# A hybrid decoder block on one core: the down projection's weights multiplied by the modulation's row during the attention and kept in DRAM; the residual's correction behind two products of the first down step

## The chip, the cores and the metric

One core of one Trainium2 chip (trn2) runs the whole block in one program. The metric is device time in microseconds (us). The engines are named as in the profile: PE (TensorE, matrix products), DVE (VectorE), ACT (ScalarE), POOL (GpSimd), SP (SyncE, here the queue that issues nearly all DMAs).

## The reference

The block has 1024 tokens of width 1024, one sequence, and everything is float32. A conditioning vector gives six rows of 1024 numbers; two of them, g1 and g2, scale what is added to the residual.

```python
cond = jax.nn.silu(c)
mod = (cond @ w_ada[l] + b_ada[l])[:, None, :]
sh1, sc1, g1, sh2, sc2, g2 = jnp.split(mod, N_ADA, axis=-1)

h = modulate(rmsnorm(x, norm1_g[l]), sh1, sc1)
u, q, k, v, gate_a, gate_b = jnp.split(h @ w_in[l], IN_SPLITS, axis=-1)
y_a = s5_branch(u, ...) @ w_a[l]
y_b = stick_breaking_attention(q, k, v) @ w_b[l]
merged = (jax.nn.sigmoid(gate_a) * y_a + jax.nn.sigmoid(gate_b) * y_b) @ w_o[l]
x = x + g1 * merged

h = modulate(rmsnorm(x, norm2_g[l]), sh2, sc2)
ffn = (jax.nn.silu(h @ w_ffn_gate[l]) * (h @ w_ffn_up[l])) @ w_ffn_down[l]
x = x + g2 * ffn
return rmsnorm(x, norm_f_g)
```

The hidden width of the FFN is 2816 = 22 x 128, so `w_ffn_down` is 22 tiles of 128 x 1024. Because g2 is a row over the output columns, `g2 * (a @ w)` equals `a @ (w * g2)`: the kernel multiplies the weights.

## The kernel before, in words

**Products in three passes.** Most float32 operands are split into a high part (a copy to a shorter float format, on ACT) and a low part (the difference, on DVE or POOL); a product is then three PE passes, high-high, high-low and low-high (`PRODUCTS`). `operand` does such a split for a tile of 128 x 1024 and takes the two result tiles from a ring that turns: two entries of pool `w`, one of `wg`, one of `wx`. In the down projection four tiles of pool `f` join the ring.

**Order.** The program is traced in Python and then ordered by a planner: an instruction may go to its engine as soon as the planner's own simulation has its inputs ready and its buffer free, earlier lines first among those that are ready. On each engine the resulting order is fixed, and an instruction that has to wait holds up everything behind it on that engine (DMA issues on SP too). In the attention the PE products are pinned to their program order (`pinned`); `self.after` adds an order between two instructions by hand.

**The attention** (`attention`) goes over 40 units, each a block of keys against 512 queries for a pair of heads: `scores` (products, then exponent and logarithm on ACT, splits on DVE at L875 to L877), `sums` (running sums over keys with a carried row, L898 to L902) and `values`. Between them PE is fed from `fillers`: 14 projections (q, k and gate) of 48 products, whose weights are loaded two projections ahead and split with the help of POOL (L454, L455).

**The modulation's columns.** The products of the conditioning vector with `w_ada` are made as partial sums per partition on DVE (`ada_rest`, L966 to L978) and stored as `aD`; the columns 8 to 11 are made in `branch_a`, 10 and 11 being g2. `ada_row` turns two such columns into a row on all partitions: load, split, products with a matrix of ones, and the bias added.

**The FFN** is one level of a seven-product scheme (Winograd's): matrices are cut into two by two blocks, sums of blocks are multiplied, and the seven products are added up with signs. `gate_up` does it for 11 pairs of hidden tiles and stores what the down projection needs of the hidden blocks as `hD`. At pair 8 it also makes the row g2 (L1178, L1179).

**The down projection** (`down`) handles the first 20 weight tiles in three steps of 4, 3 and 3 pairs (`STEPS`), each with seven products in the order (2, 4, 5, 3, 1, 6, 7); the last two tiles are added at the end, row block by row block. For each step it loads the weight tiles and multiplies them by the row on POOL:

```python
nc.sync.dma_start(out=w, in_=w_v[m])
nc.gpsimd.tensor_tensor(w, w, g2, ALU.mult)      # L1308
```

For each of the seven products and each pair, a stage tile gets the hidden block (a load from `hD`, L1329) and the sum or difference of two weight blocks (POOL, L1337), and is split by ACT and DVE (L1338, L1339). A product whose weight operand is a single block (2 and 5) needs no sum; its halves are split directly (L1334, L1335). One product of a four-pair step is 48 PE matmuls (L1354) into four banks.

The results are gathered in seven accumulators `acc`. Four of them (4, 5, 7, 6) start from the residual x, loaded from `xD` (L1295); in the first step the products 2, 3 and 1 are copied into theirs (half by ACT, half by DVE), the others are added by DVE (L1360). Since 4 and 5 also start from the residual and are later added and subtracted when the blocks are put together, accumulator 7 is corrected before: 7 plus 5 minus 4, four POOL operations on 128 x 1024 (L1298), traced ahead of the first step. In the last step POOL puts the blocks together (`closing`, L1315); the last rows are normalized and stored.

## Time and profile before

| | |
|---|---|
| median of 3 runs | 1498.04 us (1497.13 to 1499.16) |
| the profiled execution's own time | 1498.89 us |
| span of that profile | 1497.2 us |
| granted TensorE clock over the span | 0.976 |
| PE, DVE, ACT, POOL busy | 1414.6, 1125.6, 621.6, 504.3 us |

By the span's stretches: the state-space branch and the first projections to about 300 us, the merge of that branch (`branch_a`) to 370, the attention to about 668, its merge and the output product to 840, the up product of the FFN to 1253, the down projection to the end. A line of the profile such as "L1308 POOL TENSOR_TENSOR pa<-pa,row 128x1024" names the source line, the engine, the operation, the result and the operands by the program's tile names; "idle before, releaser" says how long the engine waited before it and what ended the wait. Weight tiles of the down projection are `pa`, the accumulators `pb` and `x`, the row g2 is `row`.

### The profile page before, as it was taken

How to read it: one execution, taken by the hardware profiler on the slowest of the kernel's cores; microseconds unless marked ns; L12 is line 12 of the kernel's file. 1: busy time of each engine (PE TensorE's matmuls, PEld its weight loads, DVE VectorE, ACT ScalarE, POOL GpSimd, SP SyncE). 2: the span in 40 equal slices, each digit the busy share in tenths (PEclk: the TensorE clock that was granted, in tenths of full speed). 3: DMA queues.
4: the chain of work that ended last, by engine and by line, in shares of the span. 5: the costliest groups of instructions: out<-in, count | busy, mean ns of one | idle time of the engine just before them, and what ended most of it. 6: DMA issues, size and time to landing. Idle time of an engine off the chain costs nothing.

```text
span 1497.2 us, 18257 instructions
## 1 busy us (share of the span) xinstructions
PE 1414.6 (94%) x6706; PEld 1118.1 (75%) x6706; DVE 1125.6 (75%) x1523; ACT 621.6 (42%) x804; POOL 504.3 (34%) x266
## 2 busy tenths in 40 slices
PE   5898999999999999999998799999999998999995
PEld 3678888787666666668887588888888886888774
DVE  5878995456797989868637866666666669999997
ACT  3321122632587776764236433333333333433323
POOL 1000000102111111104300245444555468888795
PEclk9999999999999999999999899999999999999998
DMA  9556665579011112136533233333333346455312
GB/s 340 134 110 163 151 175 134 158 258 333 27 49 50 35 37 77 50 106 218 183 108 107 81 106 106 106 106 106 106 106 106 106 174 220 143 160 175 100 50 113
DMA packets 180409, 193.55 MB, mean 129 GB/s; under 512 B 28636, under 2 KB 130080, under 8 KB 180320
## 3 DMA queue, kind: packets, MB, share of 16 engines
q1 hardware_dynamic: 171184, 184.86, 39.3%
q10 hardware_dynamic: 8912, 7.48, 1.8%
q8 instruction: 53, 0.87, 0.2%
q14 instruction: 36, 0.29, 0.1%
q0 software_dynamic: 224, 0.05, 0.0%
HBM read 142.40 MB, written 48.76 MB: 128 GB/s over the span
## 4 chain that ended last, share of the span: by engine, by line
PE 61%; DVE 20%; issue 6%; DMA 5%; ACT 4%; POOL 3%; SPq 0%; DVEq 0%; ACTq 0%; POOLq 0%
PE tq L1255 11%; PE mm L1255 5%; PE wo L1255 5%; PE mx L807 5%; PE mm L807 4%; PE ga L733 4%; PE tq L1354 3%; PE acc L807 2%; PE mm L1112 2%; PE mm L641 2%; DMA aw<-in_w_ada_dram 2%; PE z L807 2%; PE wo L1112 2%; PE mm L733 2%; PE tq L1112 1%
## 5 line engine op out<-in xcount | busy, mean ns | idle before, releaser
L471 POOL TENSOR_TENSOR ws<-wb 128x1024 f32<-128x1024 f32 x26 | 64.2, 2470 | 181.1 <-PE tq L1158 78.1
L455 POOL TENSOR_TENSOR wl<-ws,wh 128x1024 fp32r<-128x1024 f32 x12 | 31.2, 2601 | 161.2 <-ACT wh L452 151.8
L900 DVE TENSOR_TENSOR wa<-wa,acc 128x512 f32<-128x512 f32 (+1 forms) x80 | 47.0, 628 | 32.6 <-ACT row L898 30.2
L1308 POOL TENSOR_TENSOR pa<-pa,row 128x1024 f32<-128x1024 f32 x22 | 64.1, 2939 | 2.2 <-DMA pa<-in_w_ffn_down_dram 2.2
L294 POOL MEMSET tz<- 128x1024 f32 x4 | 3.8, 953 | 179.4 <-PE mm L641 96.7
L1246 POOL TENSOR_TENSOR f<-f,f 128x512 f32<-128x512 f32 x30 | 50.0, 1693 | 31.4 <-DVE f L1236 22.9
L872 ACT ACTIVATE ws<-wa 128x1024 f32<-128x1024 f32 (+1 forms) x40 | 39.1, 976 | 48.5 <-DVE wa L869 43.3
L471 POOL TENSOR_TENSOR wgs<-wb 128x1024 f32<-128x1024 f32 x14 | 34.6, 2474 | 72.4 <-DVE wgl L474 30.3
L877 DVE TENSOR_TENSOR wl<-ws,wh 128x1024 fp32r<-128x1024 f32 (+1 forms) x40 | 57.1, 1427 | 1.0
L977 DVE SCALAR_TENSOR_TENSOR acc<-aw,cond,acc 128x512 f32<-128x512 f32 x56 | 43.8, 782 | 7.8 <-DMA aw<-in_w_ada_dram 6.9
L875 DVE SCALAR_TENSOR_TENSOR ws<-wa,ws 128x1024 f32<-128x1024 f32 (+1 forms) x40 | 45.5, 1136 | 4.9 <-ACT ws L874 3.9
L1354 PE MATMUL tq<-f,f 128*128 128x512 f32 x156 | 48.2, 390 | 0.2 <-DVE f L1339 0.2
L1235 ACT ACTIVATE f<-f 128x1024 f32<-128x1024 f32 x22 | 23.3, 1061 | 59.8 <-DVE f L1277 30.4
L903 ACT ACTIVATE wa<-wa 128x1024 f32<-128x1024 f32 (+1 forms) x40 | 38.8, 971 | 19.5 <-DVE wa L900 18.5
L452 ACT CAST wh<-ws 128x1024 fp32r<-128x1024 f32 x24 | 25.1, 1048 | 50.7 <-PE wo L1112 24.0
L807 PE MATMUL z<-q,k 64*128 64x512 f32 (+3 forms) x192 | 42.6, 534 | 3.7 <-DVE wa L869 2.6
L1337 POOL TENSOR_TENSOR wb<-pa 128x512 f32<-128x512 f32 x23 | 40.6, 1776 | 15.7 <-DVE wxl L1335 5.5
L454 POOL TENSOR_SCALAR wh<-ws 128x1024 fp32r<-128x1024 f32 x6 | 7.4, 1238 | 105.2 <-issue 36.1
L1246 POOL TENSOR_TENSOR f<-f 128x512 f32<-128x512 f32 x20 | 42.2, 2127 | 0.0
L807 PE MATMUL mm<-wa,V 128*64 128x512 f32 (+3 forms) x192 | 39.8, 507 | 0.0
L873 ACT ACTIVATE ws<-ws 128x1024 f32<-128x1024 f32 (+1 forms) x40 | 39.0, 974 | 1.1
L874 ACT ACTIVATE ws<-ws 128x1024 f32<-128x1024 f32 (+1 forms) x40 | 38.7, 968 | 0.3
(911 smaller groups left out, 4712.3 us busy)
## 6 DMA issues: line engine op xcount, KB each, us to landing
aw<-in_w_ada_dram SPq DMA_DIRECT2D x64, 256.0 KB, 4.6
hD<-f SPq DMA_DIRECT2D x30, 512.0 KB, 2.8
ws<-in_w_in_dram SPq DMA_DIRECT2D x23, 512.0 KB, 4.9
wb<-in_w_ffn_gate_dram SPq DMA_DIRECT2D x44, 256.0 KB, 4.2
wb<-in_w_ffn_up_dram SPq DMA_DIRECT2D x44, 256.0 KB, 4.5
pa<-in_w_ffn_down_dram SPq DMA_DIRECT2D x22, 512.0 KB, 5.1
wb<-hD SPq DMA_DIRECT2D x40, 256.0 KB, 2.8
x<-in_x_dram SPq DMA_DIRECT2D x16, 512.0 KB, 7.2
```

The lines of the kernel that those rows point to most:

```text
L471: (add or nc.gpsimd).tensor_tensor(st, a, b, op)
L733: self.nc.tensor.matmul(ps, lhsT=w[a][:, k], rhs=act[h][k][:, b], start=(j == 0), stop=(j == n - 1))
L807: return self.tc.keep_in_program_order(self.nc.tensor.matmul(*args, **kw))
L875: nc.vector.scalar_tensor_tensor(st, a, 0.0, st, ALU.max, ALU.add)
L877: nc.vector.tensor_tensor(lt, st, ht.bitcast(F32), ALU.subtract)
L900: nc.vector.tensor_tensor(a[:, x, 0:f], a[:, x, 0:f], r[:, x, 0:f], ALU.subtract)
L977: nc.vector.scalar_tensor_tensor(acc, w[:, j], cj, acc, ALU.mult, ALU.add)
L1112: self.nc.tensor.matmul(ps, lhsT=mg[t // 4][k][:, a, P * (t % 4):P * (t % 4) + P], rhs=ws[k // 2][b][:, k % 2], start=k + j == 0, stop=k + ...
L1246: nc.gpsimd.tensor_tensor(o, a, b, op)
L1255: self.nc.tensor.matmul(ps, lhsT=w[x][:, q, k], rhs=self.B[i](y, k), start=(j == 0), stop=(j == 11))
L1308: nc.gpsimd.tensor_tensor(w, w, g2, ALU.mult)
L1354: nc.tensor.matmul(ps, lhsT=o[x][:, P * t:P * t + P], rhs=o[y][:, R], start=(j == 0), stop=(j == 3 * np_ - 1))
```

## The change

The row g2 is made in the attention instead of in the FFN, from the columns 10 and 11, which `branch_a` now makes first. A generator, `scaled_down`, is advanced once or twice per unit of the attention. For each half of the columns it loads the partial sums and the bias, makes the row by one float32 product with the ones and one DVE addition, and then, for each of the 22 weight tiles, loads a half tile of 128 x 512, multiplies it by the row on POOL and stores it to a scratch tensor `wD` in DRAM: 44 such steps on two buffers. `down` then loads its weights from `wD` and multiplies nothing. In the first down step the products come in the order `FIRST`, and the four corrections of accumulator 7 are traced behind its first two products, 2 and 3. The tile that holds small rows at the start lives in a pool that is closed earlier.

```diff
+FIRST = (2, 3, 1, 6, 7, 5, 4)
...
-            self.rows(const)
+            self.rows(ap)
...
-    def attention(self, qk, qp, kp, vp, op, gp, work):
+    def attention(self, qk, qp, kp, vp, op, gp, work, aside):
...
                 some(FILL[1] if i >= 0 else FILL[2])
+            for _ in range(2 if i % 8 == 0 else 1):
+                next(aside, None)
         some(10000)
+        for _ in aside:
+            pass
...
+    def scaled_down(self, pool):
+
+        nc, i = self.nc, self.i
+        w_v = i["w_ffn_down"][0].rearrange("(m p) n -> m p n", p=P)
+        for c in range(2):
+            cs = slice(512 * c, 512 * c + 512)
+            t = pool.tile([P, 512], F32, name="wd", bufs=2)
+            nc.sync.dma_start(out=t, in_=self.aD[:, 6 + c])
+            g = pool.tile([P, 512], F32, name="g2")
+            nc.sync.dma_start(out=g, in_=i["b_ada"][0, 5120 + 512 * c:5632 + 512 * c].partition_broadcast(P))
+            yield
+            ps = self.mm.tile([P, 512], F32, name="mm")
+            nc.tensor.matmul(ps, lhsT=self.ones, rhs=t, start=True, stop=True)
+            nc.vector.tensor_tensor(g, ps, g, ALU.add)
+            yield
+            for m in range(22):
+                t = pool.tile([P, 512], F32, name="wd", bufs=2)
+                nc.sync.dma_start(out=t, in_=w_v[m][:, cs])
+                nc.gpsimd.tensor_tensor(t, t, g, ALU.mult)
+                nc.sync.dma_start(out=self.wD[m][:, cs], in_=t)
+                yield
...
-            for n in ((8, 9), (10,), (11,), ())[c]:
+            for n in ((10, 11), (8,), (9,), ())[c]:
...
             if j == 8:
-                g2 = self.rp.tile([P, 1024], F32, name="row")
-                self.ada_row(g2, 6, tp, self.banks, ("ft", None))
...
-        for i, op in ((5, ALU.add), (4, ALU.subtract)):
-            for a in range(2):
-                nc.gpsimd.tensor_tensor(flat(acc[7][a]), flat(acc[7][a]), flat(acc[i][a]), op)
...
-            nc.sync.dma_start(out=w, in_=w_v[m])
-            nc.gpsimd.tensor_tensor(w, w, g2, ALU.mult)
+            nc.sync.dma_start(out=w, in_=self.wD[m])
...
-            for n, i in enumerate(ORDER):
+            for n, i in enumerate(ORDER if s else FIRST):
+                if s == 0 and n == 2:
+                    for z, op in ((5, ALU.add), (4, ALU.subtract)):
+                        for a in range(2):
+                            nc.gpsimd.tensor_tensor(flat(acc[7][a]), flat(acc[7][a]), flat(acc[z][a]), op)
```

More of the change, by code (lines that the diff above doesn't have):

```diff
@@ L1182, in ffn @@
         self.exp_ln(*self.silus)
-        self.down(const, tp, g2, gf)
+        self.down(const, tp, gf)
     def gate_up(self, pair, wv, tp):
@@ L1277, in combine, with down @@
             tt(c[0], m[7], c[0], ALU.add)
-    def down(self, const, tp, g2, gf):
+    def down(self, const, tp, gf):
         nc = self.nc
-        w_v = self.i["w_ffn_down"][0].rearrange("(m p) n -> m p n", p=P)
         x_v = self.xD.rearrange("(t p) n -> p t n", p=P)
@@ L1419, in run @@
             self.hD = dram.tile([10, P, 7, 512], F32, name="hD")
+            self.wD = dram.tile([22, P, 1024], F32, name="wD")
             self.nD = dram.tile([1024, 1024], F32, name="nD")
@@ L1468, in run @@
                     op = s3.enter_context(self.pool("o", 4))
-                    with self.pool("tri", 1) as tri, self.pool("work", 1) as work, self.pool("zp", ZPB, PSUM) as self.zp, self.pool("acc", 1, PSUM) as self.accp, \
+                    with self.pool("tri", 1) as tri, self.pool("work", 1) as work, self.pool("sc", 1) as sc, self.pool("zp", ZPB, PSUM) as self.zp, self.pool("acc", 1, PSUM) as self.accp, \
                             self.pool("mx", MXB, PSUM) as mx:
@@ L1474, in run @@
                         qk = [list(qk[0])] + [[None, None] for _ in range(3)]
-                        ops = self.attention(qk, qp, kp, vp, op, gp, work)
+                        ops = self.attention(qk, qp, kp, vp, op, gp, work, self.scaled_down(sc))
                         spare = []
```

## The prediction

> **What bounds the kernel now.** I read the page first, then the table of stretches, then the timelines around the step that the change touches.
>
> ```profile
> PE 1414.6 (94%) x6706; PEld 1118.1 (75%) x6706; DVE 1125.6 (75%) x1523; ACT 621.6 (42%) x804; POOL 504.3 (34%) x266
> ...
> L1308 POOL TENSOR_TENSOR pa<-pa,row 128x1024 f32<-128x1024 f32 x22 | 64.1, 2939 | 2.2 <-DMA pa<-in_w_ffn_down_dram 2.2
> ```
>
> PE is busy for 94% of the span, so only stretches in which PE waits are worth anything. The 64.1 us of multiplications on POOL (L1308) are a price only where something waits for them or for what they slow. The stretches (columns: length, then busy time and count for PE, PEld, DVE, ACT, POOL, then granted clock, DMA share, GB/s):
>
> ```profile
> 370.00:400.00 30.00, 27.35 (x121) 19.26 (x122) 20.01 (x24) 16.00 (x20) 8.98 (x8) 0.89 0.17 50
> ...
> 1250.00:1270.00 20.00, 13.71 (x49) 10.46 (x49) 18.86 (x15) 11.43 (x15) 15.12 (x7) 0.83 0.29 99
> 1270.00:1360.00 90.00, 89.24 (x395) 73.57 (x394) 86.59 (x71) 35.34 (x47) 70.92 (x35) 1.00 0.49 150
> 1360.00:1420.00 60.00, 58.58 (x257) 47.83 (x256) 60.00 (x55) 21.73 (x27) 49.62 (x25) 1.00 0.47 139
> ```
>
> A busy PE is not PE at its peak, so I count matmuls. The chain gives the full rate, and the PE timeline the gap:
>
> ```profile
> 1287.82 5.45 PE mm L1354 x24
> ```
>
> ```profile
> 1262.03 0.80 PE L1354 MATMUL tq<-wl,wh 128*128 128x512 f32 x1 [5.48 <-DVE wl L1335]
> ```
>
> 24 matmuls take 5.45 us, 0.227 each. The 20 us from 1250 hold 49 where 88 would go: 39 x 0.227 = **8.9 us lost** at the step from the up product to the down product. 5.48 of it is the wait for the low part of an operand (wl, L1335); most of the rest is the slow clock after it (0.83 in this stretch). From 1270 to 1420 652 matmuls x 0.227 = 148.0 of 150 us: 2.0 lost. Why was DVE late? POOL, then DVE, in time:
>
> ```profile
> 1225.36 10.45 POOL L1308 TENSOR_TENSOR pa<-pa,row 128x1024 f32<-128x1024 f32 x4
> ...
> 1239.26 10.38 POOL L1308 TENSOR_TENSOR pa<-pa,row 128x1024 f32<-128x1024 f32 x4
> ...
> 1252.99 11.23 POOL L1298 TENSOR_TENSOR pb<-pb 128x1024 f32<-128x1024 f32 x4
> ```
>
> ```profile
> 1247.30 2.88 DVE L1335 TENSOR_TENSOR wl<-pa,wh 128x512 fp32r<-128x512 f32 x1
> ...
> 1259.14 2.83 DVE L1335 TENSOR_TENSOR wl<-pa,wh 128x512 fp32r<-128x512 f32 x1
> ...
> 1271.73 0.68 DVE L1335 TENSOR_TENSOR wl<-wb,wh 128x512 fp32r<-128x512 f32 x1
> ```
>
> The same subtraction of 128x512 takes 0.68 us undisturbed and 2.8 to 2.9 beside POOL's eight multiplications and four corrections: some 2.2 us lost by each. That is the mechanism on which the change acts.
>
> **The change, part by part.** *The step into down.* The eight multiplications (10.45 + 10.38 = 20.8 us) leave this place; the four corrections (11.23) stay on POOL and only stand behind two products in the code. The planner starts what is ready, and they become ready when the residual's last blocks land:
>
> ```profile
> 1238.64 1.66 SPq L1295 DMA_DIRECT2D pb<-xD  x2
> ```
>
> ```profile
> pb<-xD SPq DMA_DIRECT2D x6, 512.0 KB, 9.5
> ```
>
> About 1240 + 9.5 = 1249.5: so I expect the corrections at 1249 to 1260, across the step, as before. Of 32.1 us of POOL's heavy work 20.8 leaves, 65%. The loss is then anything from 0 to 8.9; by that share I take 5.8 off. What is late next is the second operand pair: its tile is freed only by the last up product, because one operand less is split in the up stage (the row's) and the ring of operand tiles is shifted by one.
>
> *FIRST.* Products 3 and 1 come before those that add to the residual; half of their evictions go to ACT, so DVE has less in the first three products and more in the last four: zero in sum. The last product of the step is now 4, which reads both weights of a pair, so no tile of them is free before its sums; the next step's six loads lose some lead. Their last three in the trace:
>
> ```profile
> 1309.98 4.79 SPq L1307 DMA_DIRECT2D pa<-in_w_ffn_down_dram  x3
> ```
>
> The step's seven products of 48 matmuls, at 0.227 from 1262, end near 1338: a lead of 23 us covers it, and I cost it at nothing. Without that cover it is one landing, under 10 us by the pb<-xD row.
>
> *Later steps.* 14 more multiplications leave; DVE was full there (60.00 of 60). These rows are PE's waits from 1150 on:
>
> ```profile
> PE wo L1394 <- DVE wl L474: 2.4, 1, 2.4
> PE wo L1354 <- DVE wl L1339: 0.9, 1, 0.9
> ```
>
> Of the 2.0 lost between 1270 and 1420 I take 1.5 back (ends 0 and 2.0). The 2.4 us stand beside POOL's closing sums, not beside multiplications; DVE comes to it less late: half, 1.2 (ends 0 and 2.4).
>
> *The row's products leave the up stage.*
>
> ```profile
> 1175.90 0.39 PE L992 MATMUL mm<-wh,ones 128*128 128x512 f32 x1
> ```
>
> The first of four; at 0.227 each 0.9 us of a dense PE: minus 0.9. Their cast, split, two adds and two loads lay beside that PE: zero.
>
> *What is added in the attention.* Two fp32 products with the ones, 44 multiplications of 128x512 on POOL, two DVE adds, and on SP's queue 4 small loads, 44 loads and 44 stores. First how full the attention is:
>
> ```profile
> 395.00:645.00 250.00, 248.79 (x1138) 162.69 (x1137) 214.30 (x242) 185.28 (x213) 34.89 (x17) 1.00 0.15 48
> ```
>
> ```profile
> 479.48 1.08 PE L807 MATMUL mm<-wa,V 128*64 128x512 f32 x4
> ```
>
> PE is dense (248.79 of 250), so the two products are on the path. The nearest fp32 row, two products of 512 columns on half the array each in 1.08 us, gives 0.5 to 1.1 for one; I take the full 1.1, since a full-width one can't share the array: plus 2.1 (ends 1.1 and 2.2).
>
> POOL is nearly free there (34.89), DVE is not: 35.7 of 250 idle. A multiplication's time is that of POOL's sums of the same size; what it does to DVE is read from the splits of attention beside the POOL work that is there already (groups by shape, then two undisturbed ones):
>
> ```profile
> L1337 POOL TENSOR_TENSOR wb<-pa x23: 1284/1687/2357, 1251.3 to 1421.9; 128x512 f32<-128x512 f32 x23
> ```
>
> ```profile
> L877 DVE TENSOR_TENSOR wl<-ws,wh 128x1024 fp32r<-128x1024 f32 x22 | 36.4, 1654 | 0.6
> ...
> L876 DVE TENSOR_SCALAR wh<-ws 128x1024 fp32r<-128x1024 f32 x22 | 17.3, 786 | 0.6
> ```
>
> ```profile
> 489.44 0.69 DVE L876 TENSOR_SCALAR wh<-ws 128x1024 fp32r<-128x1024 f32 x1
> 490.17 1.23 DVE L877 TENSOR_TENSOR wl<-ws,wh 128x1024 fp32r<-128x1024 f32 x1
> ```
>
> 22 x (1.654 - 1.23) + 22 x (0.786 - 0.69) = 11.4 us of DVE delay from 34.9 us of POOL: 0.33 per us. 44 multiplications of 1.28 to 1.69 us are 56 to 74 us of POOL, so 19 to 24 us of delay against 35.7 idle. It fits, with little over. PE's price for today's 11.4 is one row:
>
> ```profile
> PE acc L807 <- DVE row L902: 1.2, 1, 1.2
> ```
>
> In proportion 2.0 to 2.6: I take plus 2.3 (ends 0 and the rival below). The Trainium skill ("SBUF — State Buffer", section "SBUF: two separate sides") says that the port pair which VectorE shares with GpSimd is an exclusive lock: whoever starts first holds it for the whole instruction. The 2.88 against 0.68 agrees; by that rule taken at its worst each multiplication costs DVE its full length, which is the slower rival.
>
> SP's queue: a store waits for its multiplication, and behind it stand the projections' weights and the gates' stores.
>
> ```profile
> gD<-gst SPq DMA_DIRECT2D x14, 256.0 KB, 2.0
> ```
>
> ```profile
> wb<-hD SPq DMA_DIRECT2D x40, 256.0 KB, 2.8
> ```
>
> The wait is at most one load and one multiplication, 2.8 + 1.7 = 4.5 us; weights are loaded two projections ahead, so zero, and 4.5 a time where that cover is gone. A step of load, multiplication, store is 2.8 + 1.7 + 2.0 = 6.5 us on one of two buffers, 3.25 a step: the 44 could be done in 143 us, and the planner does run ahead, as this load of the attention's values shows, issued long before the stretch above:
>
> ```profile
> 316.69 1.21 SPq L947 DMA_DIRECT2D V<-vD  x2
> ```
>
> The reordered columns in the merge of the state-space branch, the row tile in another pool, and reading the weights from the scratch copy instead of the input (same size): zero.
>
> **Sum**: -5.8 - 1.5 - 1.2 - 0.9 + 2.1 + 2.3 = -5.0 against the profiled execution's own 1498.89 us (span 1497.2): **1493.9 us**. The median of the runs is 1498.04, so that is 4.1 us (0.28%) under it; 0.2% (3 us) is about what a measurement of this kernel can tell from no change.
>
> **Rivals.** *A, all of it comes back.* The corrections run before or after the step; DVE is never late, and the attention hides everything: -8.9 - 2.0 - 2.4 - 0.9 + 1.1 = -13.1, 1485.8. For it: 65% of the POOL work leaves. Against: the landing at 1249.5. Chance 0.14.
>
> *B, the corrections take the multiplications' place (no change).* POOL, now free, starts them exactly at 1249.5 to 1260, when DVE must split the second pair. Two splits late by 2.15 (2.83 - 0.68) are 4.3 of PE wait; with the slow clock's some 3 us only 1.6 of the 8.9 is gained, and nothing at the end: -1.6 - 1.5 - 0.9 + 2.1 + 2.3 = +0.4, 1499.3. Chance 0.26. Whether the clock drops after a short wait decides 3 us of this:
>
> ```profile
> 376.52 1.65 PE L807 MATMUL z<-q,k 64*128 64x384 f32 x4 [2.55 <-DVE wa L869]
> ```
>
> After this wait of 2.55 us the clock did drop (0.89 in its 30 us, first row of the stretches), so I keep the 3 us. The Trainium skill ("TensorE: Matmul & The Clock Gate", section "Part 1: The HAM clock gate") puts the drop to half rate at an idle window of about 3.4 us that runs free of the work; by that rule two waits of 2.15 would be spared it, and B would end at 1496.3; a quarter of B's chance goes there.
>
> *C, slower: DVE fills up in the attention.* If the 44 are done in 143 us, DVE has 35.7 x 143 / 250 = 20.4 us idle beside them. It decides from 20.4 / 44 = 0.46 us of delay per multiplication; 0.33 x 1.28 to 1.69 is 0.42 to 0.56, right at that point. At 0.7 the overflow is 30.8 - 20.4 = 10.4 us, PE waiting for the carried row (L902): -5.0 - 2.3 + 10.4, 1502.0. Chance 0.17.
>
> *D, the order.* The second ones-product stands on PE's queue where the planner expects its input; 22 steps later than planned by 0.3 us each, PE waits 6.6: 1500.5. Chance 0.06.
>
> **How the numbers follow.** My forecast has 0.37 (own range 1490 to 1497.5). The ends of the range are A's and C's: 1486 to 1503, with about one tenth outside at each side. Faster by over 0.2% (under 1495.0): 0.29 of the forecast, all of A, some of B and C: 0.49. Within: 0.08 + most of B + a little of C and D: 0.30. Slower: the rest of C, D and B, 0.21.
>
> **What would show it.** Right: the stretch around PE's first down product holds 75 or more matmuls of 88, its wait for wl under 3 us; no L1308; DVE's splits there mostly 0.7 us. In the attention, POOL at some 91 to 109 us between the same two points, DVE's L877 mean at 2.0 to 2.4, PE's waits for L902 together under 4 us, and 2 us for the ones-products. Wrong: corrections beside the second pair's splits and a wait over 4 us (B); waits for L902 of 8 us or more with DVE full (C); one long PE wait at the ones-product (D); or closing sums that start earlier on POOL and shorten the tail behind PE's last matmul, which I put at nothing.

## The result and the profile after

The changed kernel is slower: 1510.67 us median (1506.51 to 1513.56) against 1498.6 us of the kernel before in the same series, ratio 1.009, interval 1.0068 to 1.0112. The profiled execution took 1513.56 us, its span is 1511.5 us, 14.3 us more than before. It is the slowest of the four executions, and the medians differ by 12.1 us only; what follows takes the 14.3 us of this one execution apart.

The page after, engine line and the new group:

```profile
PE 1427.3 (94%) x6706; PEld 1116.7 (74%) x6706; DVE 1110.0 (73%) x1522; ACT 620.1 (41%) x803; POOL 507.1 (34%) x288
...
L981 POOL TENSOR_TENSOR wd<-wd,g 128x512 f32<-128x512 f32 x44 | 69.2, 1578 | 86.3 <-DMA wd<-in_w_ffn_down_dram 67.8
```

The matmuls are the same 6706, yet PE is busy for 12.7 us longer: the page alone doesn't say where. So I cut the span at PE's first and last matmul of each function (attention from its first to its last product, the others up to their last; us). One profile of each kernel; the experiments below are in the same table.

| kernel | attention | merge | wo product | up product | down loop | last tiles + tail | span |
|---|---|---|---|---|---|---|---|
| before | 298.0 | 49.2 | 91.7 | 444.1 | 203.2 | 40.8 | 1497.2 |
| after | 313.2 | 49.4 | 93.4 | 448.6 | 200.0 | 36.1 | 1511.5 |
| e1 order alone | 295.6 | 47.6 | 91.7 | 444.1 | 206.3 | 40.9 | 1495.6 |
| e2 no multiplication | 298.1 | 51.0 | 93.0 | 447.8 | 200.1 | 36.1 | 1495.9 |
| e3 nothing in the attention | 297.6 | 50.9 | 92.9 | 449.4 | 200.4 | 35.8 | 1501.7 |
| e4 row tile alone | 297.0 | 50.8 | 93.0 | 450.1 | 202.6 | 40.9 | 1504.3 |
| e5 after + 32 bytes | 311.0 | 51.0 | 91.7 | 442.3 | 200.4 | 35.7 | 1503.9 |
| e6 before + 32 bytes | 295.5 | 47.6 | 92.9 | 449.3 | 202.9 | 40.7 | 1498.8 |
| e7 in the up product | 295.8 | 47.6 | 91.7 | 461.6 | 197.1 | 35.5 | 1498.7 |
| e8 the same, late corrections | 297.2 | 50.8 | 91.7 | 459.9 | 190.4 | 35.6 | 1497.8 |
| e9 paced in the attention | 307.4 | 47.9 | 92.1 | 443.0 | 190.4 | 35.7 | 1484.6 |
| e10 paced in the up product | 295.6 | 47.6 | 91.7 | 444.4 | 190.4 | 35.5 | 1478.8 |
| e11 late corrections alone | 295.5 | 49.2 | 91.7 | 444.5 | 201.5 | 40.8 | 1494.2 |
| e12 before + 64 bytes | 297.3 | 47.6 | 92.9 | 449.0 | 202.9 | 40.8 | 1500.6 |
| e13 half of e9's | 300.1 | 49.5 | 91.8 | 442.1 | 190.4 | 35.6 | 1479.5 |
| e14 e9 on DVE | 309.6 | 47.9 | 93.3 | 442.8 | 190.4 | 35.6 | 1488.6 |

Where an edit doesn't touch the attention it comes out between 295.5 and 298.0, the merge between 47.6 and 50.9: differences up to 2.5 us in the first and 3.3 us in the second say nothing. The wo product and the up product fall into two levels each (91.7 to 92.1 and 92.9 to 93.4; 442.1 to 444.5 and 447.8 to 450.1, e7 and e8 aside), and within a level of the up product kernels with the same code there differ by up to 1.6 us (after, e2, e3). One kernel crosses: e14's wo product has a wait of 1.3 us for DVE in it. The loop and the end repeat within 0.6 us where nothing in them was edited. After against before: +15.1 attention, +0.2 merge, +1.7 and +4.5 in the two products, -3.2 down loop, -4.7 at the end, +0.7 ahead of the attention (not in the table): the 14.3 of the span.

**The attention**, the stretches that the prediction shows of before (PE, PEld, DVE, ACT, POOL busy, clock, DMA share, GB/s):

```profile
370.00:400.00 30.00, 25.70 (x118) 17.71 (x119) 22.01 (x23) 15.71 (x19) 16.36 (x14) 0.94 0.50 158
395.00:645.00 250.00, 237.48 (x1077) 152.92 (x1075) 222.38 (x229) 170.75 (x197) 101.12 (x57) 1.00 0.40 128
```

1077 matmuls where 1138 stood, at full clock. PE's waits between 370 and 685 us, which were 3.7 (row) and 2.6 (wa) before:

```profile
PE acc L808 <- DVE row L903: 12.2, 12, 1.6
PE z L808 <- DVE wa L870: 5.9, 3, 3.5
```

Twelve short waits for the carried row. In all PE idles for 18.1 us of this attention (313.16 - 295.06, rows further down) against 6.3 before: 11.8 of the 15.1 us are waits. The other 3.3, in which PE counts as busy, were not taken apart. DVE's instructions from the attention's first to its last product, before and after; the sums with an operand in PSUM, where the kernel keeps PE's results (wa from acc, row from acc), stand last in each:

```profile
L877 DVE TENSOR_TENSOR wl<-ws,wh 128x1024 fp32r<-128x1024 f32 (+1 forms) x40 | 57.1, 1427 | 1.0
L875 DVE SCALAR_TENSOR_TENSOR ws<-wa,ws 128x1024 f32<-128x1024 f32 (+1 forms) x40 | 45.5, 1136 | 4.9 <-ACT ws L874 3.9
L876 DVE TENSOR_SCALAR wh<-ws 128x1024 fp32r<-128x1024 f32 (+1 forms) x40 | 28.3, 708 | 1.0
L900 DVE TENSOR_TENSOR wa<-wa,acc 128x512 f32<-128x512 f32 (+1 forms) x80 | 47.0, 628 | 32.6 <-ACT row L898 30.2 <-PE acc L807 2.4
L902 DVE TENSOR_TENSOR row<-acc,row 1x1024 fp32r<-1x1024 f32 (+2 forms) x32 | 32.4, 1014 | 1.0
```

```profile
L878 DVE TENSOR_TENSOR wl<-ws,wh 128x1024 fp32r<-128x1024 f32 (+1 forms) x40 | 61.3, 1533 | 1.1
L876 DVE SCALAR_TENSOR_TENSOR ws<-wa,ws 128x1024 f32<-128x1024 f32 (+1 forms) x40 | 55.4, 1385 | 5.4 <-ACT ws L875 4.5
L877 DVE TENSOR_SCALAR wh<-ws 128x1024 fp32r<-128x1024 f32 (+1 forms) x40 | 37.0, 924 | 1.0
L901 DVE TENSOR_TENSOR wa<-wa,acc 128x512 f32<-128x512 f32 (+1 forms) x80 | 46.9, 627 | 24.4 <-ACT row L899 22.5 <-PE acc L808 1.8
L903 DVE TENSOR_TENSOR row<-acc,row 1x1024 fp32r<-1x1024 f32 (+2 forms) x32 | 32.4, 1014 | 1.0
```

The three that read and write SBUF alone became longer by 106, 249 and 216 ns; those that read PSUM did not move by more than 1 ns.

**The step into down** in the kernel after, four stretches from shortly before it:

```profile
1255.00:1275.00 20.00, 20.00 (x88) 16.29 (x87) 15.09 (x20) 7.19 (x11) 10.29 (x6) 1.00 0.99 369
1275.00:1295.00 20.00, 14.86 (x53) 11.62 (x53) 18.95 (x11) 6.77 (x8) 18.84 (x9) 0.83 0.36 110
1295.00:1385.00 90.00, 90.00 (x395) 73.92 (x395) 70.81 (x76) 37.19 (x51) 39.78 (x24) 1.00 0.54 170
1385.00:1445.00 60.00, 60.00 (x265) 49.30 (x264) 53.27 (x57) 22.91 (x29) 33.80 (x20) 1.00 0.38 109
```

53 of 88 matmuls in the 20 us from 1275 (PE's first down product starts at 1275.3), 35 x 0.227 = 7.9 us lost against 8.9 before, again at a clock of 0.83. Its wait, and what POOL and DVE did there:

```profile
PE tq L1377 <- DVE wl L1358: 5.1, 1, 5.1
```

```profile
1268.72 2.41 POOL L1347 TENSOR_TENSOR pb<-pb 128x1024 f32<-128x1024 f32 x1 [0.79 <-DMA pb<-xD]
...
1272.74 1.78 DVE L1358 TENSOR_TENSOR wl<-pa,wh 128x512 fp32r<-128x512 f32 x1
1273.94 6.22 POOL L1347 TENSOR_TENSOR pb<-pb 128x1024 f32<-128x1024 f32 x2
1275.08 2.81 DVE L1362 TENSOR_TENSOR f<-ws,f 128x1024 fp32r<-128x1024 f32 x1
```

The corrections run at the landing of the residual, beside the splits, though they stand behind two products in the code. The later steps are dense now: 660 matmuls x 0.227 = 149.8 of the 150 us from 1295.

**The up product** has no more waits than before, but fewer matmuls in the same time. A stretch of 100 us in the middle, before and then after:

```profile
900.00:1000.00 100.00, 100.00 (x442) 82.78 (x442) 62.06 (x67) 31.29 (x35) 49.80 (x25) 1.00 0.37 119
```

```profile
920.00:1020.00 100.00, 100.00 (x436) 81.59 (x435) 60.73 (x65) 31.37 (x35) 50.70 (x25) 1.00 0.35 114
```

That was nowhere in the prediction.

### The profile page after: what moved, and what is told of

It reads as the page before. It is cut to its first block, busy times and chain, and to the rows that moved or that the text cites. A ratio compares the mean times of both kernels' runs of the same rounds, so it can differ in the third digit from the quotient of the medians.

```text
span 1511.5 us, 18475 instructions
## 1 busy us (share of the span) xinstructions
PE 1427.3 (94%) x6706; PEld 1116.7 (74%) x6706; DVE 1110.0 (73%) x1522; ACT 620.1 (41%) x803; POOL 507.1 (34%) x288
## 4 chain that ended last, share of the span: by engine, by line
PE 63%; DVE 23%; ACT 6%; DMA 5%; issue 3%; SPq 0%; POOL 0%; DVEq 0%; ACTq 0%; POOLq 0%
PE tq L1280 13%; PE mm L1280 7%; PE tq L1377 6%; PE wo L1280 6%; PE ga L734 4%; PE mm L1377 3%; PE wo L1377 3%; DVE ws L876 2%; DVE wl L878 2%; PE mm L1139 2%; PE mm L642 2%; PE mx L808 2%; DMA aw<-in_w_ada_dram 2%; DVE wa L901 2%; PE wo L1139 2%
## 5 line engine op out<-in xcount | busy, mean ns | idle before, releaser
L981 POOL TENSOR_TENSOR wd<-wd,g 128x512 f32<-128x512 f32 x44 | 69.2, 1578 | 86.3 <-DMA wd<-in_w_ffn_down_dram 67.8
L878 DVE TENSOR_TENSOR wl<-ws,wh 128x1024 fp32r<-128x1024 f32 (+1 forms) x40 | 61.3, 1533 | 1.1
L876 DVE SCALAR_TENSOR_TENSOR ws<-wa,ws 128x1024 f32<-128x1024 f32 (+1 forms) x40 | 55.4, 1385 | 5.4 <-ACT ws L875 4.5
L808 PE MATMUL acc<-wh,upto 128*128 128x512 f32 (+1 forms) x80 | 31.5, 394 | 12.2 <-DVE row L903 12.2
L808 PE MATMUL mx<-pb,wh 128*128 128x512 f32 x128 | 42.0, 400 | 0.0
L1360 POOL TENSOR_TENSOR ws<-pa 128x512 f32<-128x512 f32 x20 | 32.7, 1641 | 20.9 <-DVE f L1362 8.9
L874 ACT ACTIVATE ws<-ws 128x1024 f32<-128x1024 f32 (+1 forms) x40 | 38.9, 974 | 1.1
```

What stands on the lines that cost most here:

```text
L808: return self.tc.keep_in_program_order(self.nc.tensor.matmul(*args, **kw))
L876: nc.vector.scalar_tensor_tensor(st, a, 0.0, st, ALU.max, ALU.add)
L878: nc.vector.tensor_tensor(lt, st, ht.bitcast(F32), ALU.subtract)
L981: nc.gpsimd.tensor_tensor(t, t, g, ALU.mult)
L1360: last_sum = nc.gpsimd.tensor_tensor(st[:, R], u, W[p][b[0]][:, 512 * b[1]:512 * b[1] + 512], SIGN_B[i])
```

## Experiments

### First series: what the attention's work, the order and the row tile each do

**e1**: the kernel before with only the order and the moved corrections (the cut shows the beginning of the edit).

```diff
+            for n, i in enumerate(ORDER if s else FIRST):
+                if s == 0 and n == 2:
...
```

> The kernel before with the new order of the first down step and the corrections behind its two products, the multiplications left in the down projection. Theory B (corrections and second operand pair collide on the port that DVE shares with POOL, whatever stands before them): the step into down still loses 7 to 9 us, the tail after PE's last matmul may shorten by up to 2.6 us as in the changed kernel; 1495.5 to 1499. Rival (the order itself is what shortened the tail and the last tiles): the wait of 2.4 us for wl in the last tiles and 2.6 us of tail go here too, 1493. If the eight multiplications now run into the corrections, 1500 to 1503.

1501.61 us, ratio 1.003 (1.0012 to 1.0047), by its total the last case of the expectation. The order with the corrections behind two products, as the changed kernel has them, costs 3.1 us in the down loop (206.3) and leaves the end at 40.9. So the shorter end of the changed kernel comes from the multiplications leaving down, not from the order.

**e2**: the changed kernel without the multiplication, all else kept.

```diff
-                nc.gpsimd.tensor_tensor(t, t, g, ALU.mult)
```

> The changed kernel without the POOL multiplication: the 44 half tiles are loaded and stored unscaled (the weights' factor is left out), all transfers and the row's products stay. Theory port (POOL's multiplications slow DVE's instructions, PE waits for the carried row): the attention comes back from 313.2 to 299 to 301 us (2 us of it the two ones-products), DVE's splits L877/L878 and L876 back to the means of before (1427 and 1136 ns), total 1496 to 1498. Rival queue (88 more transfers on SP's queue and the planner's order): the attention stays at 310 or more and the total at 1508 or more.

1500.21 us, ratio 1.0016 (1.0006 to 1.0025). The attention is back at 298.1 with all 88 transfers and both row products in it, and so are the three instructions:

```profile
L878 DVE TENSOR_TENSOR wl<-ws,wh 128x1024 fp32r<-128x1024 f32 (+1 forms) x40 | 54.5, 1363 | 1.1
L876 DVE SCALAR_TENSOR_TENSOR ws<-wa,ws 128x1024 f32<-128x1024 f32 (+1 forms) x40 | 45.1, 1128 | 4.9 <-ACT ws L875 4.0
L877 DVE TENSOR_SCALAR wh<-ws 128x1024 fp32r<-128x1024 f32 (+1 forms) x40 | 25.7, 642 | 1.0
```

The rival (88 more transfers and their order) falls: they are all still there, and the 15 us are gone with the multiplications. A store's wait for its multiplication is gone too; but PE's waits in the changed kernel name DVE's row and wa, and no weight and no load. The median is 2.2 us above my band; the profiled execution, 1497.96 us, lies in it, with the two products still slow (93.0 and 447.8).

**e3**: no `scaled_down` at all, down reads the input's weights.

> The changed kernel with nothing added in the attention: no row, no multiplication, no transfers to a scratch; down reads the weights from the input, so the factor is left out. The rest of the change (order of the first step, corrections, row tile in the other pool, reordered columns) stays. Theory: attention back to 298 us; what the down part brings stays, 5.3 + 2.6 us; the up product either back at 444 us (then 1490 to 1491) or still at 448 to 449 us (then 1495 to 1496), the latter if it is the moved row tile, which shifts all tiles behind it in SBUF. Rival: the up product's slowness comes from the attention's work or the scratch, then 444.

1498.73 us, ratio 1.0 (0.9989 to 1.0011), 2.7 us over the band for this case, which nothing here explains. Attention 297.6, and the up product still 449.4: its slowness has nothing to do with the attention's work or the scratch.

**e4**: the kernel before with the one line that moves the small row tile.

```diff
-            self.rows(const)
+            self.rows(ap)
```

> The kernel before with one edit: the tile of small rows in the pool that is closed early, which shifts all tiles of the left pools by some 0.5 KB. Theory addresses: matmuls in the up product at 436 per 100 us instead of 443, up product 449 to 450 us against 444, wo products 93.6 against 91.9, total 1503 to 1505. Rival: nothing to do with it, 1498.

1506.02 us, ratio 1.0051 (1.0036 to 1.0066): this line costs 0.5% by itself. Groups of the up product by operand tiles (minimum/median/maximum ns), before and then e4:

```profile
L1255 PE MATMUL tq<-pa,wgh x80: 389/389/389, 947.4 to 1187.3; 128*128 128x512 f32 x80
L1255 PE MATMUL tq<-x,wgh x80: 389/389/389, 969.2 to 1209.0; 128*128 128x512 f32 x80
```

```profile
L1255 PE MATMUL tq<-pa,wgh x80: 389/389/397, 950.4 to 1193.7; 128*128 128x512 f32 x80
L1255 PE MATMUL tq<-x,wgh x80: 393/395/399, 972.4 to 1216.0; 128*128 128x512 f32 x80
```

wgh lies in a pool of the left side, pa too, x in a pool of the right side (`side="right"`). Sorted in this way, all groups of e4 agree: with both operands on one side a matmul starts 227 to 229 ns after the one before (group means from the trace), with operands of both sides 233. Pool wx, which lies on the right, turns the pattern round: its groups with pa and pb are at 233, those with x and f at 227 to 229. The row tile and its small neighbour take 512 + 32 bytes; without them the tiles of the left pools (pa, pb, wh, wgh) move by 544 bytes and the right ones stay.

### Second series: the remainder of the address, and another place for the multiplications

**e5**: the changed kernel with 32 unused bytes ahead of the left pools, so that they are moved by 512.

```diff
             const = es.enter_context(self.pool("const"))
+            const.tile([P, 8], F32, name="shift")
```

> The changed kernel with one unused tile of 32 bytes per partition ahead of the pools of the left side, so that they start 512 instead of 544 bytes earlier than in the kernel before. Theory alignment (a matmul whose two operands lie in pools of different sides takes 233 to 234 ns instead of 227 where the sides differ by 32 bytes modulo 128): the up product goes from 448.6 back to 443 to 444 us, the wo product from 93.4 to 91.7, all matmuls of the up product at 227 ns, total 1503 to 1505. Rival size (the 544 bytes themselves, not their remainder, or the other pool of the row tile): up product stays at 448 to 450 us, total 1509 to 1512. The attention stays at 311 to 315 us in both.

1502.33 us, ratio 1.0039 (1.0023 to 1.0054): 32 unused bytes take the ratio from 1.009 to 1.0039. The wo product is back at 91.7, the up product at 442.3, below before, where the row's four products (0.9 us by count) stood in it, and the pairs are equal:

```profile
L1280 PE MATMUL tq<-pa,wgh x64: 389/389/389, 963.1 to 1163.9; 128*128 128x512 f32 x64
L1280 PE MATMUL tq<-x,wgh x64: 389/389/389, 984.8 to 1185.6; 128*128 128x512 f32 x64
```

The attention stays at 311.0.

**e6**: the same 32 bytes in the kernel before, nothing else.

> The kernel before with one unused tile of 32 bytes ahead of the left pools and nothing else. Theory alignment: as bad as the moved row tile, up product 449 to 451 us against 444, wo product 93 against 91.7, matmuls with operands of both sides at 233 to 234 ns, total 1503 to 1506. Rival (the row tile's place in the other pool does it): no change, 1496 to 1499.

1505.09 us, ratio 1.0046 (1.003 to 1.0061); up product 449.3, and the pair of both sides is slow again:

```profile
L1255 PE MATMUL tq<-pa,wgh x80: 389/389/395, 945.0 to 1188.1; 128*128 128x512 f32 x80
L1255 PE MATMUL tq<-x,wgh x80: 395/396/397, 967.0 to 1210.3; 128*128 128x512 f32 x80
```

e5 and e6 together settle it: the same 32 bytes cure one kernel and slow the other. It is not the size of the shift and not the pool of the row tile, but how the two sides stand to each other.

**e7**: the multiplications in the up product. The row is made at pair 1, then three whole tiles are loaded, multiplied and stored at each pair.

```diff
+            for m in range(3 * j - 6, min(3 * j - 3, 22)) if j > 1 else ():
+                t = tp.tile([P, 1024], F32, name="ft")
+                nc.sync.dma_start(out=t, in_=w_v[m])
+                nc.gpsimd.tensor_tensor(t, t, g2, ALU.mult)
+                nc.sync.dma_start(out=self.wD[m], in_=t)
```

> The kernel before with the multiplications moved to the up product instead of the attention: the row made at pair 1, three whole tiles loaded, multiplied on POOL and stored to the scratch at each pair from 2 on, down loads them from there; order, corrections and row tile as before. Theory port: what counts is how full DVE is where POOL multiplies; in the up product DVE is busy for 62 of 100 us against 214 of 250 in the attention, so 22 x 2.9 = 64 us of POOL cost PE nothing there (up product 444 to 445 us, attention 298), and the down projection keeps most of the gain of the changed kernel: last tiles and tail 36 us against 40.8, step into down as before or a little better; 1489 to 1494. Rival (POOL's multiplications cost PE wherever they stand, or the transfers collide with the weights' loads): up product 450 us or more, 1498 or slower.

1502.48 us, ratio 1.0043 (1.0025 to 1.0061). The attention is untouched and the down side gains as expected (197.1, 35.5), but the up product takes 461.6. PE's waits in it from 855 us on, behind a wait of 10.1 us at its start that the kernel before has too:

```profile
PE tq L1262 <- ACT f L1269: 6.9, 2, 4.7
PE wo L1262 <- ACT f L1269: 4.8, 1, 4.8
```

These are 11.7 us in three waits; most of the rest of the 17 goes in the slower clock around them (0.96 and 0.98 in the stretches below). PE waits for an accumulator tile f that ACT is to copy a result of the product to, not for DVE's splits. ACT waits there for the stores of the hidden blocks to hD (43.3 us in four waits), which by the code stand behind the hidden sums on POOL, and on SP's queue between the loads and stores of the multiplications; which of the two held them up was not tried. The planner put 18 of the 22 multiplications into 160 us (POOL's time in them by stretches):

```profile
940.00:1020.00 80.00, 31.51 (x12) 0.96 0.78 258
1020.00:1100.00 80.00, 16.91 (x6) 0.98 0.53 176
1100.00:1260.00 160.00, 0.00 (x0) 1.00 0.42 144
```

**e8**: e7 with the order `FIRST` and the corrections tied behind the fourth product's last sum.

```diff
+                if s == 0 and n == 4:
...
+                            self.after(nc.gpsimd.tensor_tensor(flat(acc[7][a]), flat(acc[7][a]), flat(acc[z][a]), op), last_sum)
```

> As the kernel with the multiplications in the up product, with the order (2, 3, 1, 6, 7, 5, 4) in the first down step and the four corrections ordered behind the last POOL sum of its fourth product instead of at the landing of the residual. Theory B (the step into down is slow because the corrections run beside the splits of the second operand pair): the first 20 us of down hold 80 or more matmuls of 88 instead of 49, 5 to 8 us less than with the multiplications in the up product alone, 1484 to 1488. Rival (the splits wait for tiles or for loads of the hidden blocks, not for the port): the step stays where it is, within 2 us of the kernel without this edit; or the late corrections hold up the sums behind them on POOL and cost as much as they bring.

1497.52 us, ratio 1.0 (0.9986 to 1.0015), 5.0 us under e7; the total misses my band because the up product stays at 459.9. The step, in e7 and then here:

```profile
1262.90:1282.90 20.00, 18.45 (x82) 14.75 (x81) 19.90 (x14) 9.77 (x13) 13.96 (x7) 1.00 0.44 146
```

```profile
1275.00:1295.00 20.00, 20.00 (x90) 16.57 (x89) 20.00 (x14) 11.00 (x14) 17.98 (x8) 1.00 0.43 131
```

90 matmuls in the 20 us behind the step at full clock, DVE and POOL as full as ever; the view of PE's waits lists none from there to the end of down. The loop takes 190.4 us, 6.7 less than e7, and that is its 840 matmuls at 0.227: nothing is lost. But the expectation compared with the 49 of the kernel before, and e7, with the old order and the corrections at the landing, already had 82. What e7 still lost it lost mainly at its third product, by a wait of 2.6 us for a split. And e8 changes order and place at once; e5 and e9 differ in the down projection by the corrections' place alone.

### Third series: pace, and the corrections alone

**e9**: the changed kernel, the 32 bytes, the late corrections, and each load in the attention tied to the matmul that PE had reached.

```diff
-                nc.sync.dma_start(out=t, in_=w_v[m][:, cs])
+                self.after(nc.sync.dma_start(out=t, in_=w_v[m][:, cs]), self.mark)
```

> The changed kernel with the 32 bytes, the corrections behind the fourth product's last POOL sum, and each of the 44 loads in the attention ordered behind the matmul that PE had reached there, so that the multiplications come one or two per unit instead of in bunches. Theory C (what costs is that POOL's multiplications bunch up beside a DVE with no idle time left): the attention comes back from 311 to 313 us to 300 to 303, and with 12 us from the down projection the total is 1485 to 1489. Rival (each multiplication costs PE the same wherever it stands in the attention): attention 310 to 313, total 1495 to 1499.

1486.72 us, ratio 0.9925 (0.9906 to 0.9944). The multiplications now lie evenly (6 to 9 in each 50 us from 400 to 650; in the changed kernel 14, 2, 8, 13 and 3), but the attention comes back to 307.4 only. The total lies in theory C's band, the attention in neither: bunching was about a third of the price (3.6 us against e5, 5.8 against the changed kernel). In the down loop, where this kernel differs from e5 by the corrections' place alone, 200.4 became 190.4: with this order the place at the landing is the whole loss of the loop, once the multiplications are gone.

**e10**: the multiplications in the up product, in halves, one behind each product, tied to its last matmul; late corrections.

```diff
+            t = pool.tile([P, 1024], F32, name="ft")
+            self.after(nc.sync.dma_start(out=t, in_=w_v[m]), self.mark)
+            for c in (slice(0, 512), slice(512, 1024)):
+                self.after(nc.gpsimd.tensor_tensor(t[:, c], t[:, c], g[:, c], ALU.mult), self.mark)
+                yield
+            nc.sync.dma_start(out=self.wD[m], in_=t)
```

> The multiplications in the up product as before, but in halves of 128x512, one behind each product of the pairs 2 to 8, each ordered behind that product's last matmul, with the late corrections. Theory pace (in the bunched form 22 multiplications on POOL between 940 and 1100 us held up the hidden sums on the same engine and PE waited 22 us for f): up product back to 444 to 447 us, total 1482 to 1486. Rival (the multiplications cost the up product 16 us by contention however they are spread): 458 or more, 1496 to 1499.

1479.88 us, ratio 0.9879 (0.986 to 0.9898): the fastest of all, 1.2% under the kernel before and 2 us under the theory's band. Of the 22 us of waits that the expectation names, 10.1 stand in the kernel before too, and 10.3 still here. The up product is at 444.4 with all 44 half multiplications in it:

```profile
L1196 POOL TENSOR_TENSOR ft<-ft,row 128x512 f32<-128x512 f32 x44 | 75.6, 1736 | 23.0 <-issue 11.9 <-DMA ft<-in_w_ffn_down_dram 9.4 <-POOL f L1263 0.8
```

75.6 us of POOL, and the up product is 0.3 us longer than before, which is within its scatter. So e7 lost its 17 us to the form, not to the work: e10 spreads the multiplications and halves each, and which of the two did more was not taken apart.

**e11**: the kernel before with the order and the late corrections alone.

> The kernel before with the multiplications left where they were; only the order of the first down step and the corrections behind the fourth product's last POOL sum. Theory (corrections and multiplications each hold DVE up on their own): some 5 to 7 us of the step into down come back, the last tiles and the tail stay at 40.8 us; 1490 to 1493. Rival (without the corrections the eight multiplications still make the step late, or the late corrections now queue behind the second step's multiplications): 1495 to 1500.

1496.76 us, ratio 0.9986 (0.9973 to 0.9998), in the rival's band. The loop goes from 203.2 to 201.5 only: beside the multiplications the order and the late place together are worth 1.7 us, without them 6.7 (e7 to e8). PE still waits for splits, 2.1, 2.2 and 2.1 us at 1256, 1281 and 1316. The loop's lengths of all kernels, side by side, take the three parts of the change apart (190.4 is a loop in which nothing is lost):

| down loop, us | old order, corrections at the landing | `FIRST`, at the landing | `FIRST`, late |
|---|---|---|---|
| with multiplications | 202.6 to 203.2 (before, e4, e6, e12) | 206.3 (e1) | 201.5 (e11) |
| without | 197.1 (e7) | 200.0 to 200.4 (after, e2, e3, e5) | 190.4 (e8, e9, e10, e13, e14) |

The multiplications' leaving is worth 6 us in either order with the corrections at the landing, and 11 with the late ones. `FIRST` costs 3 us with or without the multiplications, as long as the corrections stay at the landing; why was not tried.

**e12**: the kernel before with 64 unused bytes.

> The kernel before with one unused tile of 64 bytes ahead of the left pools: both sides then differ by 64 bytes modulo 128 and by none modulo 64. If the matmul's slowness goes by the remainder modulo 64, nothing changes: up product 444 us, 227 ns everywhere, 1496 to 1499. If it goes by 128 or more, matmuls with operands of both sides take 233 to 234 ns again, up product 449 to 450 us, 1503 to 1506.

1504.69 us, ratio 1.0055 (1.0033 to 1.0077); up product 449.0, so the remainder counts modulo 128 or more, not 64:

```profile
L1255 PE MATMUL tq<-pa,wgh x80: 387/389/398, 947.3 to 1190.0; 128*128 128x512 f32 x80
...
L1255 PE MATMUL tq<-x,wh x40: 394/394/394, 900.3 to 1206.6; 128*128 128x512 f32 x40
```

### Fourth series: what the attention's price goes by

**e13**: e9 with every second multiplication left out.

```diff
+                if m % 2 == 0:
                     nc.gpsimd.tensor_tensor(t, t, g, ALU.mult)
```

> As the kernel with the multiplications paced in the attention, but only every second of the 44 half tiles is multiplied (the others are stored unscaled). Theory price per multiplication (every us by which DVE is delayed in the attention costs PE a share of it, since the delayed splits stand in the chain from scores to sums): half the price, attention 301 to 304 us against 307.4 with all 44 and 298.1 with none, total 1481 to 1484. Rival threshold (DVE's idle time absorbs the delay until it is used up, some 36 us before): the price is gone or nearly so, attention 297 to 299.5.

1484.78 us, ratio 0.9922 (0.9908 to 0.9935). Attention 300.1, between the two bands: inconclusive, and 2.0 us over e2 is within the scatter. The whole kernel is not measurably faster than e9 (0.9925).

**e14**: e9 with the multiplication on DVE.

```diff
-                nc.gpsimd.tensor_tensor(t, t, g, ALU.mult)
+                nc.vector.tensor_tensor(t, t, g, ALU.mult)
```

> As the kernel with the multiplications paced in the attention, but DVE itself multiplies instead of POOL. If POOL's use of the SBUF port beside DVE is what costs, DVE's other instructions go back to their means of before (splits 1427, 1137, 708 ns against 1467, 1239, 919), and what is left is 44 x 0.69 = 30 us more work on DVE (286 of 298 us): attention 302 to 310. Rival (DVE's own time is worse than POOL's interference, since it fills the engine that was the second fullest): 312 or more.

1490.32 us, ratio 0.9963 (0.995 to 0.9975). Attention 309.6, in the band. The three instructions are back:

```profile
L879 DVE TENSOR_TENSOR wl<-ws,wh 128x1024 fp32r<-128x1024 f32 (+1 forms) x40 | 51.7, 1292 | 0.9
L877 DVE SCALAR_TENSOR_TENSOR ws<-wa,ws 128x1024 f32<-128x1024 f32 (+1 forms) x40 | 45.0, 1125 | 3.1 <-ACT ws L876 2.3
L878 DVE TENSOR_SCALAR wh<-ws 128x1024 fp32r<-128x1024 f32 (+1 forms) x40 | 28.0, 701 | 0.3
```

So it is POOL's work in SBUF beside them that makes them long. But spending 44 multiplications of DVE's own time costs PE about as much (309.6 against 307.4): the attention has no room for all of this work on either engine.

## Why the prediction was wrong

1493.9 was predicted, 1486 to 1503 as the range; 1510.67 came. Step by step:

- **DVE in the attention, +2.3: the step that failed.** Its first half held in size. DVE's busy time from the attention's first to its last product, before, after, e2 and e9:

```profile
370.10:668.13 298.03, 291.74 (x1315) 192.09 (x1316) 245.86 (x278) 214.72 (x246) 42.68 (x24) 0.99 0.16 50
```

```profile
370.78:683.94 313.16, 295.06 (x1318) 190.97 (x1319) 269.51 (x279) 213.48 (x246) 112.56 (x68) 0.99 0.39 124
```

```profile
369.87:667.98 298.11, 292.31 (x1318) 192.17 (x1319) 241.91 (x279) 215.08 (x246) 42.49 (x24) 0.99 0.41 130
```

```profile
368.19:675.64 307.45, 295.54 (x1318) 191.66 (x1319) 260.80 (x279) 212.46 (x244) 110.44 (x68) 0.99 0.40 126
```

  269.51 - 245.86 = 23.7 us of delay, where 19 to 24 was worked out. That it came out so well is partly luck: I had counted two kinds of instructions, and the largest part, 9.9 us, fell on a third that I had left out (L875, 45.5 to 55.4). The splits that were to grow to 2.0 to 2.4 us, 1654 ns before, did not grow at all (stretch from 395 to 660):

```profile
L878 DVE TENSOR_TENSOR wl<-ws,wh 128x1024 fp32r<-128x1024 f32 x22 | 34.1, 1549 | 0.6
```

  What failed is the price: I took today's one wait of 1.2 us over today's 11.4 us of delay, 0.1 us of PE per us. Measured is 15.1 over 23.7, 0.6, in bunches, and against e2 (307.4 - 298.1) over (260.80 - 241.91), 0.5, evenly spread. The stretch from 395 to 645 from which I took the wait had cut two more off: the whole attention shows 3.7 us in three, but in proportion even these give only 7.7. Nor is it one price per us: against e2, e13's 10.9 us of DVE time cost 2.0 and e14's 30.0 cost 11.5. A price from one wait in a place where the delay is mostly hidden can't be carried in proportion to a place where it is three times as long; and DVE's idle time (52 us of 298) was no reserve, since after it still idles for 44 of 313 and PE waits all the same. By the code the delayed instructions stand in the chain from scores to sums, and each sum waits for the row carried from the one before; the waits for the row (12.2 us) fit that.
- **Rivals C and D.** C had the wait (L902, now L903: 12.2 us), and my line for it, 8 us or more, was passed; "DVE full" was not. Its 0.7 us of delay per multiplication came from no row, and 23.7 / 44 = 0.54 was measured, which by C's own rule is an overflow of 3.3 us. It put the whole price on the bunching, at 1502.0; e9 shows that spreading takes back 4 to 6 us. Whether a price per multiplication or a threshold stands behind the rest is open: e13 fell between. D's wait at the ones-product is in no row.
- **The row tile in another pool: zero, without a reason given.** Wrong by 1.7 + 4.5 us in the two products, or more: the up product also lost its row's 0.9, and e5, with the same products and the right remainder, is at 442.3, so the up product's part is 6.3. This alone would have taken the prediction to 1501.9. Nothing in the trace of before could show it, but two kernels with shifted pools are not the same kernel, and I gave the line no bounds.
- **The step into down, -5.8.** Measured -1.0 (7.9 lost against 8.9), with corrections beside late splits and a wait of 5.1 us. These are rival B's signs, and its price for the step, 1.6 gained, came close. That was in part luck, for the -1.0 is two things at once. With the old order the multiplications' leaving brings 6.1 us in the loop (203.2 to 197.1, e7), near the 7.3 that I had taken for the step and the later steps together; the step then holds 82 of 88 matmuls, and most of what is still lost is lost at the third product, so the share of POOL's work came near in size and not in place. `FIRST` then took 3 us back. I had put "no change" on B as a whole and so saw B and C as rivals; they came together.
- **FIRST at nothing.** With the corrections at the residual's landing it costs 3.1 us beside the multiplications (e1) and 2.9 to 3.3 without them (e7 against after, e2, e3 and e5): a term of +3 that I had left out. Only together with the late corrections does it pay.
- **Later steps, -1.5.** Lost before 2.0, after 0.2: -1.8. Right.
- **Last tiles, -1.2, and the tail at nothing.** Together -4.7: the wait of 2.4 is gone, and the end behind PE's last matmul went from 16.4 to 13.8. POOL's last closing sums in before and after:

```profile
1472.92 4.77 POOL L1315 TENSOR_TENSOR pb<-pb,x 128x512 f32<-128x512 f32 x3
```

```profile
1485.52 4.78 POOL L1334 TENSOR_TENSOR pb<-pb,x 128x512 f32<-128x512 f32 x3
```

  They end at 1477.7, 3.1 us ahead of PE's last matmul (1497.2 - 16.4 = 1480.8), and after at 1490.3, 7.4 us ahead (1511.5 - 13.8 = 1497.7). That they start earlier was named as what would make the zero wrong. The gain in the two together stands in every kernel that keeps the multiplications out of down, and in none that keeps them there.
- **Row's products, -0.9 and +2.1.** Consistent: in the kernels without them the up product is 1.1 to 2.0 under before (e5, e9, e13, e14); in the attention each half of the row takes two records of 0.592 us that start 0.43 us apart, so some 0.86 us, 1.7 for both:

```profile
374.50 1.02 PE L975 MATMUL mx<-wd,ones 128*128 128x512 f32 x2
```

  and e2, which has both halves, is within the scatter of before. SP's queue at nothing: right by e2 and by PE's waits, none of which is for a load.

The sum, with what was measured in place of what I took, in the prediction's order: -1.0 - 1.8 - 4.7 with the tail, about 15 for the attention with its row products, 6 for the shifted pools with the row's 0.9 in it, is +13.5 of the 14.3; the 3 us of `FIRST` are inside the -1.0.

## What to carry to other kernels

Moving work off a busy place is worth as much as the place where it goes has room, and room is not an engine's idle share alone: find the chain there that the delayed instructions stand in, and bound the price by all of the delay, not in proportion to a wait that happens to be seen today. In the up product, whose products by the code do not wait for one another and where DVE is also emptier (62 of 100 us busy against 214 of 250), work spread evenly on POOL was nearly free; which of the two reasons makes it so was not separated. The same work in bunches of whole tiles cost 17 us there. An order that is costed at nothing, like `FIRST`, wants a run of its own as much as the work that is moved. And an edit that changes an allocation by a few bytes is an edit of its own: count matmuls per 100 us in a stage that the change doesn't touch.

## What the runs showed of the hardware

- **Matmul operands on different sides.** A matmul of 128x512, one of a product's three passes, went from 227 ns to mostly 233 from start to start (229 to 231 in some groups of e12; in the rows' medians from 389 to 393 to 396 ns) where stationary and moving operand lay in pools whose addresses differ by 32 or 64 bytes modulo 128 (e4, e6, e12), and not where the difference is a multiple of 128 (before, e5). Operands in pools of one side kept 227 to 229, and down, where both operands of a product come from the same pool, was not touched (202.6 to 202.9 against 203.2). Which other multiples of 128 are free besides the 512 of e5, and what lies behind it, was not tried.
- **POOL beside DVE.** 44 multiplications of 1578 ns made DVE's three kinds of instructions that use SBUF alone longer by 22.8 us in all (4.2 + 9.9 + 8.7), a third of POOL's 69.2 us, and its instructions with a PSUM operand by nothing (628 and 627 ns, 1014 and 1014). The Trainium skill ("SBUF — State Buffer", section "SBUF: two separate sides") states that DVE meets the lock in a two-port mode, or with two SBUF inputs against a GpSimd operation that reads SBUF. By that rule DVE's sums with one operand in PSUM go free, and the trace agrees. Its full length for each multiplication, the worst case that the prediction weighed, would have been 69 us; the trace shows a third.
